# Rotary steps of q and k moved ahead of their squares, and convolution taps alternated in a transformer block

## The chip, the cores and the metric

The kernel runs on one core of one Trainium2 chip. The metric is the device time of one execution in microseconds (us); for the kernel before it is the median of three runs. The engines are TensorE (PE in the profile; PEld is its weight load), VectorE (DVE), ScalarE (ACT), GpSimd (POOL) and SyncE (SP), which here issues the transfers of weights.

## The reference

One block of a hybrid network on a sequence of 256 rows of 2048 elements, in fp32: a modulation vector from `c`, a first feed-forward network (hidden width 5632), a mixer, and a second feed-forward network, each behind a normalisation and with a gated residual. The change lies in the mixer, cut here to what matters:

```python
proj = h @ w_in                        # 256 x 5120: q, k, v, conv_a, conv_g
q = apply_rope(rms_norm(q, q_norm), cos, sin)     # 8 heads x 2 maps x 64
k = apply_rope(rms_norm(k, k_norm), cos, sin)
attn = diff_attention(q, k, v, lam)    # softmax of map 0 minus lam * softmax of map 1
u = conv_a * sigmoid(conv_g)           # 256 x 1024
u = causal_depthwise_conv(u, conv_w, conv_b)      # 31 taps for each channel
u = silu(layer_norm(u))
out = concat(attn, u) @ w_out
```

## The kernel before

**Tiles of weights.** Each product with a weight matrix is made from tiles of 512 rows by 512 columns, laid out as 128 partitions x 2048. SP loads such a tile as `raw`; `w_tile` splits it in two halves of 128x1024. Of each half ACT casts a high part `whi` (L299), and DVE takes the rest, `wlo` = `raw` - `whi` (L301). PE then makes three matmuls of 128x512 for each quarter of the tile and each half `t` of the 256 rows: `whi` with the activation's high part (L323), `wlo` with that part (L327), and `whi` with the activation's low part (L328). A tile is thus 4 x 2 x 3 = 24 matmuls. `raw`, `whi` and `wlo` have four buffers each.

**The mixer.** The projection by `w_in` goes through ten chunks of 512 columns, `ci` = 0 to 9: four of the convolution, then q0, k0, q1, k1 (each half of the heads' maps) and v0, v1. A chunk is four tiles, `pc` = 0 to 3, summed into two accumulators in PSUM, one for each `t`. What follows a finished chunk is issued by `finish_mix` behind the first tile of the next one.

- For a q or k chunk that is `qk_chunk`. For each `t`, ACT makes eight squares with row sums of 128x64 from the accumulator (L908), `rstd_of` turns the sums into `rs` (DVE scales them, L147; POOL raises them to a power, L148). DVE makes the rotary step: a product with the cosines (L913), two half products with the sines (L918), and their sum (L920). For k, ACT then scales the eight heads by `rs` (L923); for q, `rs` goes into the softmax later. One tile of weights later PE transposes the result (L895), and ACT copies it out (L898 for q, L900 and L901 for k). The scores of attention (PE L946 and L949, in `attn_probs`) need the copies of k.
- For a convolution chunk, `conv_chunk` makes `u` for two tiles of 128 channels, and one tile of weights later its inner function `rest` transposes and copies it and puts the taps into the queue `bg`. A **plain tap** is one DVE instruction that multiplies and adds for one tile of channels (L838); the tap with delay 0 is made on ACT and starts the sum (L836). A **wide tap** serves four channel tiles at once: four products on ACT (L846) and one addition of 128 x 4 x up to 256 on DVE (L848). There are eight channel tiles in two blocks of four, and in each block 8 of the 31 taps are wide (`WIDE`).

**What sets the order.** `fill(n)` takes work from `bg` up to `n` units: `TAPS[ci]` units behind every tile of chunk `ci`, where a plain tap is 1 and a wide tap 3. `after_tiles(1, f)` runs `f` one tile of weights later. A scheduler then orders the instructions of each engine from these, by the order in which they are written and by what they depend on; inside `tc.high_priority(offset=SOONER)`, with `SOONER` = 150, instructions count as written that much earlier. At run time each engine goes through its own list in that fixed order, and an instruction that waits holds up all those behind it on its engine.

Of the kernel before, what the change touches and what calls it, by code (L numbers as in the profile page):

```python
# [20 lines left out]
AF = mybir.ActivationFunctionType  # L21
# [3 lines left out]
P = 128  # L25
D = 2048
S = 256
NT = 2
# [5 lines left out]
DH = 64  # L34
CK = 31
# [3 lines left out]
SOONER = 150  # L39
# [9 lines left out]
DUE = ((8, 4), (16, 6), (22, 8), (57, 16), (108, 24), (151, 32))  # L49


TAPS = (6, 5, 6, 6, 6, 6, 8, 6, 6, 6)
TAPS_OUT = 12
WIDE = tuple(range(CK - 9, CK - 1))
RMS_EPS = 1e-6
LN_EPS = 1e-5
LAM_INIT = 0.8 - 0.6 * float(np.exp(-0.3 * 0))
# [20 lines left out]
def block_kernel(ctx: ExitStack, tc: tile.TileContext, x_in, pos_in, w_ada, small, w_gu1, w_dn1,  # L78
                 w_in, w_out, w_gu2, w_dn2, out):
    nc = tc.nc  # L80
# [57 lines left out]
    for i in range(4):  # L138
        pc = acc_tile()
        for j in range(4):  # L140
            k = 4 * i + j
# [3 lines left out]
    def rstd_of(ss, n, count, eps):  # L145

        nc.vector.tensor_scalar(out=ss, in0=ss, scalar1=1.0 / count, scalar2=eps, op0=ALU.mult, op1=ALU.add)  # L147
        nc.gpsimd.tensor_tensor(out=ss, in0=ss, in1=half[:, :n], op=ALU.pow)  # L148


    bg = deque()

    def fill(n):
        while n > 0 and bg:
            units, fn = bg.popleft()
            fn()
            n -= units
# [7 lines left out]
    def after_tiles(n, fn):  # L165
        later.append([n, fn])
# [660 lines left out]
    def conv_tap(cc, i, j):  # L827
        ct = 2 * cc + i
        y = ytile[ct // 4][:, ct % 4, :]
        p0 = _COLS["convw"][0] + ct * CK + j  # L830
        w = cst[:, p0:p0 + 1]
        d = CK - 1 - j
        u = uT[cc][:, i, :S - d]
        if d == 0:
            b0 = _COLS["convb"][0] + ct
            nc.scalar.activation(out=y, in_=u, func=AF.Identity, scale=w, bias=cst[:, b0:b0 + 1])  # L836
        else:
            nc.vector.scalar_tensor_tensor(out=y[:, d:], in0=u, scalar=w, in1=y[:, d:], op0=ALU.mult, op1=ALU.add)  # L838

    def conv_wide(b, j):  # L840

        d = CK - 1 - j
        pr = blk([P, 4, S])
        for i in range(4):
            p0 = _COLS["convw"][0] + (4 * b + i) * CK + j
            nc.scalar.activation(out=pr[:, i, d:], in_=uT[2 * b + i // 2][:, i % 2, :S - d], func=AF.Identity,  # L846
                                 scale=cst[:, p0:p0 + 1])
        nc.vector.tensor_add(out=ytile[b][:, :, d:], in0=pr[:, :, d:], in1=ytile[b][:, :, d:])  # L848

    def conv_chunk(cc, accs):  # L850
        us = []
        for t in range(NT):
            sg = tmp([P, 256])
            nc.scalar.activation(out=sg, in_=accs[t][:, 256:], func=AF.Sigmoid)
            u = tmp([P, 256])
            nc.vector.tensor_mul(out=u, in0=accs[t][:, :256], in1=sg)
            us.append(u)

        def rest():
            tp = tp_tile((P, 2, S))  # L860
            for t in range(NT):
                for i in range(2):
                    nc.tensor.transpose(tp[:, i, t * P:(t + 1) * P], us[t][:, i * P:(i + 1) * P], ident)
            uT[cc] = blk([P, 2, S])
            nc.scalar.copy(out=uT[cc], in_=tp)
            if cc % 2:
                for i in range(2):
                    bg.append((0, lambda i=i: conv_tap(cc, i, CK - 1)))
                for j in WIDE:
                    bg.append((3, lambda j=j: conv_wide(cc // 2, j)))  # L870
            for j in reversed(range(CK)):
                for i in range(2):
                    if j not in WIDE and not (cc % 2 and j == CK - 1):
                        bg.append((1, lambda i=i, j=j: conv_tap(cc, i, j)))

        after_tiles(1, rest)

    qT, kz, vv, rq_of = {}, {}, {}, {}

    def qk_chunk(name, g, accs):  # L880
        gc, gs = gcs["qn" if name == "q" else "kn"]
        if name == "q":
            dst = blk([P, 4, S])
            qT[g] = dst
        else:
            dst = [blk([P, 4, S]) for _ in range(2)]
            nc.gpsimd.memset(dst[0][DH:, :, :], 0.0)
            nc.gpsimd.memset(dst[1][:DH, :, :], 0.0)
            kz[g] = dst

        def transposed(t, A):
            tp = tp_tile((P, 4, P))
            Af = A.rearrange("p h d -> p (h d)")
            for i in range(4):
                nc.tensor.transpose(tp[:, i, :], Af[:, i * P:(i + 1) * P], ident)  # L895
            ts = slice(t * P, (t + 1) * P)
            if name == "q":
                nc.scalar.copy(out=dst[:, :, ts], in_=tp)  # L898
            else:
                nc.scalar.copy(out=dst[0][:DH, :, ts], in_=tp[:DH])  # L900
                nc.scalar.copy(out=dst[1][DH:, :, ts], in_=tp[DH:])  # L901

        for t in range(NT):
            a3 = accs[t].rearrange("p (h d) -> p h d", d=DH)
            sq = tmp([P, 8, DH])
            rs = sm([P, 8], "rs8")
            for i in range(8):
                nc.scalar.activation(out=sq[:, i, :], in_=a3[:, i, :], func=AF.Square, accum_out=rs[:, i:i + 1])  # L908
            rstd_of(rs, 8, DH, RMS_EPS)
            if name == "q":  # L910
                rq_of[g, t] = rs
            A = tmp([P, 8, DH])
            nc.vector.tensor_mul(out=A, in0=a3, in1=gc[:, t, :].unsqueeze(1).to_broadcast([P, 8, DH]))  # L913
            B = tmp([P, 8, DH])
            for h2 in range(2):
                o = slice(32 * h2, 32 * h2 + 32)
                r = slice(32 - 32 * h2, 64 - 32 * h2)
                nc.vector.tensor_mul(out=B[:, :, o], in0=a3[:, :, r],  # L918
                                     in1=gs[:, t, o].unsqueeze(1).to_broadcast([P, 8, 32]))
            nc.vector.tensor_add(out=A, in0=A, in1=B)  # L920
            if name == "k":
                for i in range(8):
                    nc.scalar.activation(out=A[:, i, :], in_=A[:, i, :], func=AF.Identity, scale=rs[:, i:i + 1])  # L923
            after_tiles(1, lambda t=t, A=A: transposed(t, A))
# [185 lines left out]
    for ci in range(10):  # L1110
        p0 = 1 if ci < HOLD else 0
        accs = first[ci][2] if ci < HOLD else [acc_tile() for _ in range(NT)]
        for pc in range(p0, 4):
            if ci == 0 and pc < 3:
                for t in range(NT):
                    st.piece(pc + 1, t)
            w = w_tile(w_in[ci, pc], ci == 0 and pc <= PRE)
            if ci == 1 or ci == 0 and pc > 1:
                ada_share(1.0, 104)
            mm_tile(accs, w, act, 4 * pc, pc == 0, pc == 3)  # L1120
            if pc == p0:
                while pend:
                    finish_mix(*pend.pop(0))
            if pc == 3 and ci < 4:
                conv_chunk(ci, accs)
            fill(TAPS[ci])
            for _ in range(UNITS):
                if probs:
                    attn_probs(*probs.popleft())
                if avq:  # L1130
                    attn_av(*avq.popleft())
        if ci >= 4:
            pend.append((ci, accs))
# [20 lines left out]
    accs = {}  # L1154
# [115 lines left out]
```

## Time and profile before

| what | value |
|---|---|
| runs | 1847.14, 1847.22, 1847.72 us; median 1847.22 |
| the profiled execution | 1849.98 us, its span 1848.2 us, mean granted clock 0.998 |
| PE busy | 1822.8 us, 99% of the span |
| DVE, ACT, POOL busy | 1438.5, 934.0, 30.2 us |

Times in the trace are counted in us from the start of the span. The stretch from 780 to 1160 us holds most of the mixer; q0 is handed to DVE and ACT at 875 us, k0 at 902 us. In a line of the timeline the columns are start, time from start to end, engine, line, operation, output <- inputs, shape, how many follow each other (x4), and in brackets the idle time ahead of it and who ended that. Instructions of an engine overlap at their ends: the time from one start to the next is shorter than the time of one.

### The profile page before, as it was taken

Reading aid. Unit: us, or ns where it says so; the run is one execution under the profiler, and the core shown is the slowest. Engines: PE = TensorE matmul, PEld = TensorE weight load, DVE = VectorE, ACT = ScalarE, POOL = GpSimd, SP = SyncE. Lnnn points to the kernel's source line nnn. Section 1 sums busy time; section 2 is a strip of 40 time slices with the busy share of each in tenths; the row PEclk is TensorE's granted clock in tenths of the full one; section 3 lists DMA queues with packets and bytes.
Section 4 is the critical chain, followed back from the end, with each engine's and each line's share of the span. In section 5 each row is a group of like instructions: output and inputs, shape, how many; then the busy total and the mean of one; then the engine's idle time right before and its main releaser. Section 6 shows DMA issues by size and latency. Waiting matters only on the chain.

```text
span 1848.2 us, 21920 instructions
## 1 busy us (share of the span) xinstructions
PE 1822.8 (99%) x8247; PEld 1502.6 (81%) x8247; DVE 1438.5 (78%) x1880; ACT 934.0 (51%) x1439; POOL 30.2 (2%) x29
## 2 busy tenths in 40 slices
PE   7999999999999999999999999999999999999999
PEld 5788888888888887788788888888888888888887
DVE  7889869998898777898998768878877765544443
ACT  7554344444444434567798655664444444433332
POOL 0000000000000000000111000000000000000000
PEclk9999999999999999999999999999999999999999
DMA  9988978889899898775444457888777755555552
GB/s 377 349 308 301 348 263 319 328 317 333 321 340 362 339 356 330 273 254 179 163 156 160 167 220 297 334 335 315 279 278 277 275 189 196 182 210 211 199 211 80
DMA packets 72729, 495.91 MB, mean 268 GB/s; under 512 B 8192, under 2 KB 8624, under 8 KB 15152
## 3 DMA queue, kind: packets, MB, share of 16 engines
q1 hardware_dynamic: 72624, 494.53, 72.2%
q8 instruction: 64, 1.05, 0.2%
q14 instruction: 41, 0.34, 0.1%
HBM read 492.37 MB, written 2.12 MB: 268 GB/s over the span
## 4 chain that ended last, share of the span: by engine, by line
PE 89%; DVE 5%; ACT 2%; DMA 1%; issue 1%; POOL 0%; SPq 0%; POOLq 0%; DVEq 0%; ACTq 0%
PE acc L327 29%; PE acc L328 29%; PE acc L323 29%; DVE wlo L301 2%; DVE blk L838 1%; PE tp L658 1%; DMA blk<-in_w_gu_dram 1%; ACT whi L299 1%; PE acc L946 1%; ACT blk L846 1%; PE tp L388 0%; DVE raw L187 0%; DMA raw<-in_w_dn_dram 0%; DMA blk<-in_w_ada_dram 0%; ACT tmp L923 0%
## 5 line engine op out<-in xcount | busy, mean ns | idle before, releaser
L299 ACT CAST whi<-raw 128x1024 fp32r<-128x1024 f32 (+1 forms) x605 | 626.8, 1046 | 711.8 <-PE acc L328 563.1
L301 DVE TENSOR_TENSOR wlo<-raw,whi 128x1024 fp32r<-128x1024 f32 (+1 forms) x605 | 724.7, 1212 | 304.4 <-ACT whi L299 303.4
L327 PE MATMUL acc<-wlo,blk 128*128 128x512 f32 x2437 | 951.8, 391 | 6.3 <-DVE wlo L301 6.2
L323 PE MATMUL acc<-whi,blk 128*128 128x512 f32 x2440 | 951.8, 393 | 1.5 <-ACT blk L397 1.3
L328 PE MATMUL acc<-whi,blk 128*128 128x512 f32 x2437 | 950.8, 390 | 0.1
L327 PEld LDWEIGHTS acc<-wlo,blk 128*128 128x128 f32 x2437 | 458.3, 188 | 103.8 <-DVE wlo L301 10.4
L323 PEld LDWEIGHTS acc<-whi,blk 128*128 128x128 f32 x2440 | 458.7, 188 | 96.0 <-ACT blk L397 1.7
L328 PEld LDWEIGHTS acc<-whi,blk 128*128 128x128 f32 x2437 | 457.8, 188 | 96.3 <-DVE blk L399 0.7
L187 DVE CUSTOM_DVE_ANT_0 raw<-raw,c_bc 128x2048 f32<-128x2048 f32 x142 | 324.3, 2286 | 15.7 <-DMA raw<-in_w_ada_dram 15.4
L486 ACT COPY blk<-acc 128x512 f32<-128x512 f32 x72 | 41.8, 588 | 61.2 <-PE acc L328 58.6
L838 DVE SCALAR_TENSOR_TENSOR blk<-blk,cst,blk 128x245 f32<-128x245 f32 (+21 forms) x176 | 70.6, 460 | 0.6 <-ACT blk L836 0.5
L650 DVE TENSOR_TENSOR blk<-acc,blk 128x512 f32<-128x512 f32 x88 | 56.7, 683 | 0.0
L323 PE MATMUL acc<-blk,blk 128*128 128x512 f32 x120 | 47.5, 398 | 1.8 <-ACT blk L315 1.8
L327 PE MATMUL acc<-blk,blk 128*128 128x512 f32 x116 | 45.3, 391 | 0.2 <-DVE blk L301 0.2
L328 PE MATMUL acc<-blk,blk 128*128 128x512 f32 x116 | 45.2, 391 | 0.0
L301 DVE TENSOR_TENSOR blk<-raw,blk 128x1024 fp32r<-128x1024 f32 x28 | 33.7, 1220 | 2.4 <-ACT blk L299 2.4
L651 ACT ACTIVATE blk<-blk 128x256 f32<-128x256 f32 x88 | 32.5, 411 | 2.9 <-DVE blk L650 2.9
L652 DVE TENSOR_TENSOR blk<-blk 128x256 f32<-128x256 f32 x88 | 33.4, 418 | 0.0
L299 ACT CAST blk<-raw 128x1024 fp32r<-128x1024 f32 x28 | 28.8, 1048 | 8.4 <-DMA raw<-in_w_dn_dram 7.1
L345 DVE TENSOR_TENSOR blk<-tp,blk 128x512 fp32r<-128x512 f32 x44 | 29.9, 684 | 0.3 <-ACT blk L344 0.3
L446 ACT ACTIVATE tmp<-tp,ada,scales 128x128 f32<-128x128 f32 x36 | 14.7, 456 | 28.0 <-DVE scales L229 15.6
L323 PEld LDWEIGHTS acc<-blk,blk 128*128 128x128 f32 x120 | 22.8, 190 | 6.6 <-ACT blk L315 2.2
(162 smaller groups left out, 739.8 us busy)
## 6 DMA issues: line engine op xcount, KB each, us to landing
raw<-in_w_gu_dram SPq DMA_DIRECT2D x161, 1024.0 KB, 5.4
raw<-in_w_ada_dram SPq DMA_DIRECT2D x142, 1024.0 KB, 6.5
raw<-in_w_dn_dram SPq DMA_DIRECT2D x88, 1024.0 KB, 4.9
raw<-in_w_in_dram SPq DMA_DIRECT2D x40, 1024.0 KB, 4.8
raw<-in_w_out_dram SPq DMA_DIRECT2D x16, 1024.0 KB, 4.8
raw<-in_w_gu_dram SPq DMA_DIRECT2D x8, 768.0 KB, 5.8
blk<-in_w_gu_dram SPq DMA_DIRECT2D x10, 512.0 KB, 13.5
blk<-gate_line SPq DMA_DIRECT2D x6, 512.0 KB, 5.5
```

The source lines that it names most:

```text
L187: nc.vector.tensor_tensor_reduce(out=raw, in0=raw, in1=c_bc, scale=1.0, scalar=0.0, op0=ALU.mult, op1=ALU.add, accum_out=ada_cols[g][:, j ...
L299: nc.scalar.copy(out=hi[:, :m, :], in_=rw)
L301: nc.vector.tensor_sub(out=lo[:, :m, :], in0=rw, in1=hi[:, :m, :].bitcast(F32))
L323: nc.tensor.matmul(acc, ah, wh, start=start, stop=False)
L327: nc.tensor.matmul(acc, ah, wl, start=False, stop=False)
L328: return nc.tensor.matmul(acc, al, wh, start=False, stop=stop)
L345: nc.vector.tensor_sub(out=lo, in0=tp, in1=hi.bitcast(F32))
L486: last_part[0] = nc.scalar.copy(out=parts[c][:, t, :], in_=accs[t])
L650: nc.vector.tensor_add(out=p[:, t, :], in0=accs[t], in1=p[:, t, :])
L651: nc.scalar.activation(out=p[:, t, :256], in_=p[:, t, :256], func=AF.Silu)
L652: nc.vector.tensor_mul(out=p[:, t, 256:], in0=p[:, t, :256], in1=p[:, t, 256:])
L838: nc.vector.scalar_tensor_tensor(out=y[:, d:], in0=u, scalar=w, in1=y[:, d:], op0=ALU.mult, op1=ALU.add)
```

## The change

Three things are edited.

1. **Rotary first.** The rotary step becomes a function `rotated`, called ahead of the squares for each `t` and inside `high_priority(offset=SOONER)`.
2. **Taps.** In the first block of four channel tiles 12 taps are wide, in the second 8 as before. The taps of a chunk are queued in one list by delay: behind plain taps number 2, 5, 8, ... stands one wide tap (in the chunks that complete a block), and it counts 2.6 units. The taps with delay 0 no longer have a place of their own at the front; they come first in that list.
3. **Units.** `TAPS` holds two numbers for each chunk: units behind its first tile, and behind each other tile.

```diff
-TAPS = (6, 5, 6, 6, 6, 6, 8, 6, 6, 6)
+TAPS = ((6, 6), (5, 5), (6, 6), (6, 7), (7, 7), (2, 7), (2, 7), (2, 7), (2, 7), (4, 7))
-WIDE = tuple(range(CK - 9, CK - 1))
+WIDE = (tuple(range(CK - 13, CK - 1)), tuple(range(CK - 9, CK - 1)))
...
-            if cc % 2:
-                for i in range(2):
-                    bg.append((0, lambda i=i: conv_tap(cc, i, CK - 1)))
-                for j in WIDE:
-                    bg.append((3, lambda j=j: conv_wide(cc // 2, j)))
-            for j in reversed(range(CK)):
-                for i in range(2):
-                    if j not in WIDE and not (cc % 2 and j == CK - 1):
-                        bg.append((1, lambda i=i, j=j: conv_tap(cc, i, j)))
+            wide = WIDE[cc // 2]
+            plain = [(i, j) for j in reversed(range(CK)) for i in range(2) if j not in wide]
+            for n, (i, j) in enumerate(plain):
+                bg.append((1, lambda i=i, j=j: conv_tap(cc, i, j)))
+                if cc % 2 and n % 3 == 1 and n // 3 < len(wide):
+                    bg.append((2.6, lambda j=wide[n // 3]: conv_wide(cc // 2, j)))
...
         for t in range(NT):
             a3 = accs[t].rearrange("p (h d) -> p h d", d=DH)
+            with tc.high_priority(offset=SOONER):
+                A = rotated(t, a3)
             sq = tmp([P, 8, DH])
             rs = sm([P, 8], "rs8")
             for i in range(8):
                 nc.scalar.activation(out=sq[:, i, :], in_=a3[:, i, :], func=AF.Square, accum_out=rs[:, i:i + 1])
             rstd_of(rs, 8, DH, RMS_EPS)
             if name == "q":
                 rq_of[g, t] = rs
-            A = tmp([P, 8, DH])
...
-            if name == "k":
+            else:
                 for i in range(8):
                     nc.scalar.activation(out=A[:, i, :], in_=A[:, i, :], func=AF.Identity, scale=rs[:, i:i + 1])
             after_tiles(1, lambda t=t, A=A: transposed(t, A))
...
-            fill(TAPS[ci])
+            fill(TAPS[ci][pc > p0])
```

In the changed kernel the lines below the edits stand elsewhere: the cast is L300, `wlo` L302, the matmuls L324, L328, L329, the plain tap L839, the wide tap's products L847 and its sum L849, the transposes L893, the rotary step L903, L908, L910, the squares L920, `rstd_of` L148 and L149, the scaling of k L926, the copies L898 and L899.

**DVE behind q0.** In the kernel before, the two parts of the tile that PE works on while q0 is worked on, `wlo_6892` and `wlo_6896`, stand just ahead of these rows, with the first `rs` (L147) between; `wlo_6969` at their end is the first part of the tile behind it:

```order
L913 TENSOR_TENSOR tmp_6935<-acc_6705,gc_qn 128x512
L918 TENSOR_TENSOR tmp_6937<-acc_6705,gs_qn 128x8x32 x2
L838 SCALAR_TENSOR_TENSOR blk_5906<-blk_6417,cst,blk_5906 128x241
L920 TENSOR_TENSOR tmp_6935<-tmp_6935,tmp_6937 128x512
L147 TENSOR_SCALAR rs_1261_6942<-rs_1261_6942 128x8
L913 TENSOR_TENSOR tmp_6953<-acc_6706,gc_qn 128x512
L918 TENSOR_TENSOR tmp_6955<-acc_6706,gs_qn 128x8x32 x2
L838 SCALAR_TENSOR_TENSOR blk_5906<-blk_6417,cst,blk_5906 128x241
L920 TENSOR_TENSOR tmp_6953<-tmp_6953,tmp_6955 128x512
L838 SCALAR_TENSOR_TENSOR blk_5906<-blk_6417,cst,blk_5906 128x240 x2
L838 SCALAR_TENSOR_TENSOR blk_5906<-blk_6417,cst,blk_5906 128x239 x2
L301 TENSOR_TENSOR wlo_6969<-raw_6965,whi_6967 128x1024
```

In the changed kernel `wlo_6920` and `wlo_6924` are the two parts of the tile that PE works on while q0 is worked on:

```order
L302 TENSOR_TENSOR wlo_6920<-raw_6916,whi_6918 128x1024
L849 TENSOR_TENSOR blk_5906<-blk_6899,blk_5906 128x4x253
L903 TENSOR_TENSOR tmp_6951<-acc_6715,gc_qn 128x512
L908 TENSOR_TENSOR tmp_6953<-acc_6715,gs_qn 128x8x32 x2
L839 SCALAR_TENSOR_TENSOR blk_5906<-blk_6417,cst,blk_5906 128x230
L910 TENSOR_TENSOR tmp_6951<-tmp_6951,tmp_6953 128x512
L903 TENSOR_TENSOR tmp_6969<-acc_6716,gc_qn 128x512
L908 TENSOR_TENSOR tmp_6971<-acc_6716,gs_qn 128x8x32 x2
L839 SCALAR_TENSOR_TENSOR blk_5906<-blk_6417,cst,blk_5906 128x229
L910 TENSOR_TENSOR tmp_6969<-tmp_6969,tmp_6971 128x512
L839 SCALAR_TENSOR_TENSOR blk_5906<-blk_6417,cst,blk_5906 128x229
L302 TENSOR_TENSOR wlo_6924<-raw_6916,whi_6922 128x1024
```

Before, both parts of the tile stood ahead of the rotary step; now the second part stands behind all of it and three plain taps, and `rs` behind that.

**ACT behind k0**, from the squares of the first `t` to the first copy of k, before:

```order
L908 ACTIVATE tmp_7137,rs_1291_7138<-acc_6886 128x64 x8
L299 CAST whi_7206<-raw_7200 128x1024
L908 ACTIVATE tmp_7163,rs_1295_7164<-acc_6887 128x64 x8
L299 CAST whi_7306<-raw_7304 128x1024
L923 ACTIVATE tmp_7149<-tmp_7149,rs_1291_7138 128x64 x8
L299 CAST whi_7310<-raw_7304 128x1024
L923 ACTIVATE tmp_7175<-tmp_7175,rs_1295_7164 128x64 x8
L299 CAST whi_7410<-raw_7408 128x1024
L299 CAST whi_7414<-raw_7408 128x1024
L900 COPY blk_7133<-tp_7234 64x4x128
```

And now; the `acc` of a square is the accumulator that DVE's rotary step reads too, and in the changed program the squares wait for DVE's L908 of the same `t`:

```order
L920 ACTIVATE tmp_7174,rs_1297_7175<-acc_6914 128x64 x8
L300 CAST whi_7330<-raw_7328 128x1024
L926 ACTIVATE tmp_7168<-tmp_7168,rs_1297_7175 128x64 x8
L920 ACTIVATE tmp_7200,rs_1301_7201<-acc_6915 128x64 x8
L300 CAST whi_7334<-raw_7328 128x1024
L926 ACTIVATE tmp_7194<-tmp_7194,rs_1301_7201 128x64 x8
L300 CAST whi_7433<-raw_7431 128x1024
L300 CAST whi_7437<-raw_7431 128x1024
L898 COPY blk_7164<-tp_7259 64x4x128
```

The squares of the second `t` now stand behind the scaling of the first. On DVE, behind k0, the order is now:

```order
L302 TENSOR_TENSOR wlo_7138<-raw_7130,whi_7136 128x1024
L903 TENSOR_TENSOR tmp_7168<-acc_6914,gc_kn 128x512
L908 TENSOR_TENSOR tmp_7170<-acc_6914,gs_kn 128x8x32 x2
L839 SCALAR_TENSOR_TENSOR blk_5907<-blk_6554,cst,blk_5907 128x241
L910 TENSOR_TENSOR tmp_7168<-tmp_7168,tmp_7170 128x512
L903 TENSOR_TENSOR tmp_7194<-acc_6915,gc_kn 128x512
L908 TENSOR_TENSOR tmp_7196<-acc_6915,gs_kn 128x8x32 x2
L148 TENSOR_SCALAR rs_1297_7175<-rs_1297_7175 128x8
L839 SCALAR_TENSOR_TENSOR blk_5907<-blk_6554,cst,blk_5907 128x240
L910 TENSOR_TENSOR tmp_7194<-tmp_7194,tmp_7196 128x512
```

Before, L147 of each `t` stood ahead of that `t`'s rotary step; now the first one stands behind the products of both. At k1, PE makes two of the first `t`'s four transposes right behind the first two matmuls of the second tile (`wlo_7854`); before, all eight stood behind that tile:

```order
L324 MATMUL acc_7751<-whi_7852,blk_5956 128x512
L324 MATMUL acc_7752<-whi_7852,blk_5956 128x512
L893 MATMUL tp_7884<-cst,tmp_7791 128x128 x2
L328 MATMUL acc_7751<-wlo_7854,blk_5956 128x512
L329 MATMUL acc_7751<-whi_7852,blk_5957 128x512
```

So these two now stand 22 matmuls earlier than the rest.

More of the change, by code (lines that the diff above doesn't have):

```diff
@@ L901, in transposed, with rotated @@
                 nc.scalar.copy(out=dst[1][DH:, :, ts], in_=tp[DH:])
[L903 to L911, printed above, removed]
+        def rotated(t, a3):
             A = tmp([P, 8, DH])
@@ L920, in qk_chunk @@
             nc.vector.tensor_add(out=A, in0=A, in1=B)
-            if name == "k":
+            return A
+        for t in range(NT):
+            a3 = accs[t].rearrange("p (h d) -> p h d", d=DH)
+            with tc.high_priority(offset=SOONER):
+                A = rotated(t, a3)
+            sq = tmp([P, 8, DH])
+            rs = sm([P, 8], "rs8")
+            for i in range(8):
+                nc.scalar.activation(out=sq[:, i, :], in_=a3[:, i, :], func=AF.Square, accum_out=rs[:, i:i + 1])
+            rstd_of(rs, 8, DH, RMS_EPS)
+            if name == "q":
+                rq_of[g, t] = rs
+            else:
                 for i in range(8):
```

## Prediction

> **What bounds the kernel now.** The page comes first: how busy each engine is. Then the windows of the mixer, where the whole change lies; then the waits of PE in them.
>
> ```profile
> span 1848.2 us, 21920 instructions
> PE 1822.8 (99%) x8247; PEld 1502.6 (81%) x8247; DVE 1438.5 (78%) x1880; ACT 934.0 (51%) x1439; POOL 30.2 (2%) x29
> ```
>
> PE is busy for 99% of the span, and no matmul is added or taken away. So the change can win only what PE now loses, or make it lose more. The second row says the same of the mixer: over 780 to 1160 us, in slices of 10 us, the sum is
>
> ```profile
> sum 380.00, PE 375.65 PEld 310.35 DVE 325.86 ACT 260.90 POOL 26.78; mean PE 9.89 PEld 8.17 DVE 8.58 ACT 6.87 POOL 0.70
> ```
>
> PE is without work for 380 - 375.65 = 4.35 us there. The slices around q0 show where (columns: window, length, busy time of PE, PEld, DVE, ACT, POOL, granted clock, DMA share, GB/s):
>
> ```profile
> 860.00:870.00 10.00, 10.00 (x45) 8.26 (x44) 7.84 (x8) 9.83 (x21) 0.00 (x0) 1.00 0.33 120
> 870.00:880.00 10.00, 9.96 (x44) 7.95 (x43) 10.00 (x22) 6.92 (x36) 1.77 (x2) 1.00 0.45 147
> 880.00:890.00 10.00, 8.19 (x34) 6.47 (x33) 10.00 (x19) 5.50 (x9) 3.42 (x3) 0.83 0.45 167
> ```
>
> At 880 to 890 us PE loses 1.81 us, has 34 matmuls where a full slice has 45, and its granted clock is 0.83; DVE is full. PE's waits in 780 to 1160 us (total, times, longest):
>
> ```profile
> PE acc L327 <- DVE wlo L301: 2.0, 2, 1.8
> PE tp L388 <- DVE tmp L380: 0.9, 2, 0.6
> PE acc L985 <- ACT blk L929: 0.7, 1, 0.7
> PE acc L323 <- ACT blk L1078: 0.3, 1, 0.3
> PE acc L946 <- ACT blk L900: 0.3, 1, 0.3
> ```
>
> Those that the change can touch are the first, 2.0 us, of which 1.8 behind q0, and the last, 0.3 us at the scores behind k1; the timeline adds about 0.3 us at the scores behind k0 (below). Together 2.6 us. The others belong to norms and to attention's end, whose instructions stay.
>
> Next, DVE and PE behind q0 (timeline):
>
> ```profile
> 875.05 2.36 DVE L301 TENSOR_TENSOR wlo<-raw,whi 128x1024 fp32r<-128x1024 f32 x2
> 877.32 0.17 DVE L147 TENSOR_SCALAR rs<-rs 128x8 f32<-128x8 f32 x1
> 877.39 0.69 DVE L913 TENSOR_TENSOR tmp<-acc,gc_qn 128x512 f32<-128x512 f32 x1
> 877.99 0.75 DVE L918 TENSOR_TENSOR tmp<-acc,gs_qn 128x256 f32<-128x256 f32 x2
> 878.65 0.47 DVE L838 SCALAR_TENSOR_TENSOR blk<-blk,cst,blk 128x241 f32<-128x241 f32 x1
> 879.03 0.69 DVE L920 TENSOR_TENSOR tmp<-tmp,tmp 128x512 f32<-128x512 f32 x1
> 879.63 0.17 DVE L147 TENSOR_SCALAR rs<-rs 128x8 f32<-128x8 f32 x1
> ...
> 883.47 2.36 DVE L301 TENSOR_TENSOR wlo<-raw,whi 128x1024 fp32r<-128x1024 f32 x2
> ```
>
> ```profile
> 875.67 0.61 PE L323 MATMUL acc<-whi,blk 128*128 128x512 f32 x2
> ...
> 879.63 0.39 PE L327 MATMUL acc<-wlo,blk 128*128 128x512 f32 x1
> 879.86 0.39 PE L328 MATMUL acc<-whi,blk 128*128 128x512 f32 x1
> ...
> 881.90 1.03 PE L895 MATMUL tp<-cst,tmp 128*128 128x128 f32 x8
> 884.75 0.50 PE L327 MATMUL acc<-wlo,blk 128*128 128x512 f32 x1 [1.81 <-DVE wlo L301]
> ...
> 885.90 0.63 PE L323 MATMUL acc<-whi,blk 128*128 128x512 f32 x1
> 886.33 0.63 PE L327 MATMUL acc<-wlo,blk 128*128 128x512 f32 x1
> ```
>
> From start to start, DVE takes 1.13 us for a `wlo` (2.27 for two), 0.60 for L913 and for L920, 0.66 for the two L918, 0.38 for a tap. PE takes 0.23 us for a matmul, so 5.44 for a tile of 24. DVE reached the next tile's first `wlo` at 883.47 only, behind the rotary step and six taps; PE had nothing else. Behind that wait the spacing is 0.43 us (885.90 to 886.33), about seven matmuls long: 7 x 0.2 = 1.4 us more. So q0 costs about 1.8 + 1.4 us today.
>
> **The change part by part.**
>
> *Taps.* Four more wide taps in the first block take away 16 plain ones: DVE saves 16 x 0.38 = 6.1 us and pays four sums, ACT pays 16 products:
>
> ```profile
> 860.52 6.48 ACT L846 ACTIVATE blk<-blk,cst 128x252 f32<-128x252 f32 x16
> 862.25 1.21 DVE L848 TENSOR_TENSOR blk<-blk,blk 128x1008 f32<-128x1008 f32 x1 [0.85 <-ACT blk L846]
> ```
>
> The sums are 4 x 1.2 = 4.8 us of DVE, the products 6.5 us of ACT. Neither lies on the path: in the slice of these very rows ACT is busy 9.83 of 10 us with sixteen products in one piece, and PE still 10.00. What covers them is tiles that are cast ahead; alternating with plain taps, the products now come four at a time. I cost them at nothing, between -0.2 us (the small wait of the second `wlo`) and +1.5 us, one group of four products (6.48 / 4 = 1.6 us) ahead of a cast that PE needs.
>
> *Rotary first, q0.* Let R be the time at which the accumulators are ready (875.19, where ACT began its squares) and E the start of the next tile on PE, 875.67. By the order now, DVE makes `wlo` for the tile's first half, a wide sum, the whole rotary step with three taps, and only then `wlo` for its second half. From the first product that is 2 x (0.60 + 0.66 + 0.38 + 0.60) + 0.38 + 1.13 = 6.0 us. PE can do 12 matmuls, two more with `whi`, and eight transposes meanwhile: 14 x 0.23 + 0.87 = 4.04 us from E (the transposes' 0.87 from their 1.03 us less the overlap). The first product starts at R at the earliest, 0.48 us before E, which makes the wait 6.0 - 0.48 - 4.04 = 1.5 us; if the first `wlo` and the wide sum run past E by 0.9 us, it is 2.9. I take a start at E + 0.3, and so 2.3 us in place of 1.8. The wait moves from the next tile into this one; it does not go.
>
> *Rotary first, k0.* Here before's rows are
>
> ```profile
> 901.90 0.22 ACT L908 ACTIVATE tmp<-acc 128x64 f32<-128x64 f32 x1 [0.98 <-PE acc L328]
> ...
> 903.49 1.10 ACT L299 CAST whi<-raw 128x1024 fp32r<-128x1024 f32 x1
> ...
> 906.96 2.11 ACT L923 ACTIVATE tmp<-tmp,rs 128x64 f32<-128x64 f32 x8
> 908.88 1.12 ACT L299 CAST whi<-raw 128x1024 fp32r<-128x1024 f32 x1
> 910.37 2.03 ACT L923 ACTIVATE tmp<-tmp,rs 128x64 f32<-128x64 f32 x8 [0.37 <-DVE tmp L920]
> 912.30 2.21 ACT L299 CAST whi<-raw 128x1024 fp32r<-128x1024 f32 x2
> 914.42 0.57 ACT L900 COPY blk<-tp 64x512 f32<-64x512 f32 x1
> ```
>
> ```profile
> 904.00 1.64 POOL L148 TENSOR_TENSOR rs<-rs,half 128x8 f32<-128x8 f32 x1 [20.46 <-DVE rs L147]
> ```
>
> ```profile
> 913.27 1.03 PE L895 MATMUL tp<-cst,tmp 128*128 128x128 f32 x8
> ...
> 914.60 0.40 PE L328 MATMUL acc<-whi,blk 128*128 128x512 f32 x1
> 915.14 0.46 PE L946 MATMUL acc<-blk,blk 128*128 128x128 f32 x2
> ```
>
> Eight squares take 1.6 us (901.90 to 903.49), eight scalings 1.9, a cast 0.95; from L147 over POOL to ACT it is about 2.0 us. PE was just not held by the transposes, and by 0.3 us at the scores (914.60 to 915.14, less one matmul). Now, with DVE starting at 901.9: the products of the first `t` end at 903.2, its squares at 904.9, but its `rs` stands behind the second `t`'s products: 901.9 + 2 x (0.60 + 0.66) + 0.38 + 0.60 = 905.4. POOL answers at 907.4; the scaling takes until 909.4. Only then come the squares of the second `t`, until 910.95; `rs` and POOL until 913.0; its scaling until 915.0. PE wants the second four transposes at 913.27 + 0.43 = 913.7 and waits 1.3 us. The copies of k come behind two casts: 915.0 + 1.9, and the first is there at 917.5. PE, 0.45 us of transposes and four matmuls after 915.1, wants it at 916.4: 1.1 us. Sum 2.4 in place of 0.3. Less if ACT's list has slack that the rows don't show: 0 at the least; more by 0.9 if DVE starts late, as at q0.
>
> *q1* now makes both parts of the tile first: 0.1 in place of 0.2. *k1*: two transposes are wanted two matmuls into the second tile, 5.44 + 0.45 after its start and so 6.4 us after R. The first scaling ends, as at k0, 909.4 - 901.9 = 7.5 us after R: 1.1 us. The other six stand 22 matmuls later (5.0 us), about when the second scaling ends; the first pair's delay helps them. 1.1 to 2.3 us; I take 1.7 in place of 0.3.
>
> *Sum.* 2.3 + 2.4 + 0.1 + 1.7 = 6.5 us against 2.6: +3.9. One slowed stretch of 1.4 us stays, as today. The profiled execution's 1849.98 us would become 1853.9; it was 2.8 above the median, so from the median 1847.2 + 3.9 = 1851.1.
>
> **Where a rule would say otherwise.** The slice at 880 us shows 0.83 of the clock behind a wait of only 1.81 us. The Trainium skill, "TensorE: Matmul & The Clock Gate", section "HAM oscillation — how this bites in real kernels", has "no PE-idle gaps >~3.4µs" as the rule for keeping the clock. By that rule no wait named here would cost any clock; the row at 880 us is against it.
>
> **The rivals.**
> - *The clock holds.* Each wait costs its own length, since none of those at k is over 1.4 us and the one at q0 may fall otherwise. Then 1.4 us goes: 1849.7. For it: the many shorter waits at clock 1.00; against it: q0's wait gets longer, and 1.81 us was enough.
> - *The clock falls more often.* Behind k0, two waits of 1.3 and 1.1 us lie within 4 us, and behind k1 as well: one or two more stretches, 1852.5 or 1853.9. For it: the row at 880 us. Against it: no such fall in before at the scores of k0 and k1, where the waits were 0.3.
> - *Not slower: the scaling of k is in time.* The price of k rests on when the second scaling ends against 913.7. If it ends 1.3 us earlier, because DVE gives `rs` ahead of the second products or ACT overlaps its small instructions better, k0 and k1 stay at 0.3 each, and the sum is 2.3 + 0.3 + 0.1 + 0.3 = 3.0: 1847.6. If q0's wait is then the 1.5 us of its lower end and takes no clock along, it is 1847.6 - 0.8 - 1.4 = 1845.4. For it: before, DVE was idle 1.65 us for the first `rs` of k0; now it starts that much earlier:
>
> ```profile
> 903.68 0.17 DVE L147 TENSOR_SCALAR rs<-rs 128x8 f32<-128x8 f32 x1 [1.65 <-ACT tmp L908]
> ```
>
>   Against it: the order, in which the squares of the second `t` stand behind the scaling of the first.
> - *Wide taps crowd the casts.* 1.5 us at one or two places in the third and fourth chunks: 1852.6 to 1854.1. Against it: the slice at 860 us.
>
> **How the numbers follow.** 0.2% is 3.7 us, about what a measurement of this kernel can tell from no change: below 1843.5 is faster, above 1850.9 slower. The forecast, 1851.1, has 0.40, and lies so near the bound that half of it is slower. The clock holds 0.14 (same), falls more often 0.18 (slower), the scaling of k in time 0.22 (0.14 same; 0.08 for a gain beyond 1843.5, if q0's wait goes as well and other waits with it), crowding 0.06 (slower). That is faster 0.08, same 0.20 + 0.14 + 0.14 = 0.48, slower 0.20 + 0.18 + 0.06 = 0.44. The range goes from 1845.4, the lower end of the k rival, to 1854.5, two more slow stretches with 0.6 us more at q0.
>
> **What would show it.** Right: PE waits inside the first tile behind q0, at L328 for the second `wlo` (L302), of about 2.3 us; at the transposes L893 behind k0, for ACT's L926, about 1.3; at the scores L949, for L898, about 1.1; at k1's first two transposes over 1. Wrong: no wait at L893; DVE's `rs` (L148) of k0 less than 3 us after the first product; or PE waiting for casts (L300) among the convolution's chunks. A gain of over 3.7 us would mean that PE lost more in the mixer than the waits above show.

## The result, and where the time went

The changed kernel takes 1861.72 us (median of six runs, 1858.56 to 1864.99) beside 1847.47 of the kernel before: the ratio estimated from the runs is 1.007, 95% interval 1.0059 to 1.0082. It is slower, the direction of the forecast, but by 14 us and not by 4, and above the range, which ended at 1854.5. The six runs form two groups, 1858.56 to 1859.23 and 1864.21 to 1864.99; the profile is of a run of the second.

The page after, its first two rows:

```profile
span 1862.9 us, 21928 instructions
PE 1828.1 (98%) x8247; PEld 1504.7 (81%) x8247; DVE 1435.6 (77%) x1868; ACT 941.0 (51%) x1455; POOL 36.7 (2%) x29
```

DVE's work fell and ACT's rose by a few us, as the taps say. The odd one is POOL: 36.7 us in place of 30.2, with the same 29 instructions. PE has more to wait for. Its waits from 860 to 1000 us, q0 to k1 (total, times, longest):

```profile
PE tp L893 <- ACT tmp L926: 7.8, 2, 4.9
PE tp L893 <- DVE tmp L910: 1.6, 1, 1.6
PE acc L328 <- DVE wlo L302: 0.8, 1, 0.8
PE acc L949 <- ACT blk L898: 0.3, 1, 0.3
```

That is 10.5 us in place of 2.3 in the same stretch of before. 1.6 and 0.8 are q0. The 7.8 are the transposes of k0 (2.9) and k1 (4.9), for ACT's scaling, and 0.3 the scores behind k0. The windows show what else that cost (window, length, busy time of PE, PEld, DVE, ACT, POOL, granted clock, DMA share, GB/s):

```profile
880.00:890.00 10.00, 7.61 (x30) 5.85 (x29) 10.00 (x17) 8.60 (x33) 5.28 (x3) 0.83 0.42 135
...
910.00:920.00 10.00, 7.13 (x31) 5.14 (x30) 5.94 (x14) 7.11 (x34) 3.48 (x2) 0.88 0.30 105
920.00:930.00 10.00, 9.73 (x45) 7.82 (x44) 7.13 (x23) 8.24 (x22) 0.00 (x0) 0.77 0.36 116
...
970.00:980.00 10.00, 4.97 (x16) 3.52 (x15) 5.62 (x9) 3.83 (x18) 6.69 (x2) 0.83 0.31 105
```

At 970 to 980 us PE made 16 matmuls where a full slice has 45. From 973.4 to 974.9 us DVE, ACT and PE all stand idle, and only POOL works, which is busy for 6.69 us of the slice. Between 860 and 1000 us the granted clock is under 0.9 at three places (880, 910 to 930 and 970 us), before at one. The profiled runs differ by 1864.99 - 1849.98 = 15.0 us. The longer waits are 10.5 - 2.3 = 8.2 of them; and PE's busy time rose by 5.3 us (1828.1 from 1822.8) with as many instructions, which is matmuls at the lower clock and transposes that come at the pace of the scaling. The remaining 1.5 us were not followed.

So the question is what ACT waited for. ACT's scalings behind k0, and then POOL's powers (start, time, in brackets the idle time ahead and who ended it):

```profile
911.73 2.03 ACT L926 ACTIVATE tmp<-tmp,rs 128x64 f32<-128x64 f32 x8 [3.95 <-POOL rs L149]
917.46 2.02 ACT L926 ACTIVATE tmp<-tmp,rs 128x64 f32<-128x64 f32 x8 [1.17 <-POOL rs L149]
```

```profile
907.10 4.59 POOL L149 TENSOR_TENSOR rs<-rs,half 128x8 f32<-128x8 f32 x1 [15.94 <-DVE rs L148]
...
969.79 5.11 POOL L149 TENSOR_TENSOR rs<-rs,half 128x8 f32<-128x8 f32 x1 [13.82 <-DVE rs L148]
```

The same power over 128x8 that took 1.64 or 1.65 us at q0, k0, q1 and k1 of before takes 4.59 and 5.11 for the first halves of k0 and k1; the second halves take 1.78 and 1.79. What DVE did beside the one at k1:

```profile
969.48 0.17 DVE L148 TENSOR_SCALAR rs<-rs 128x8 f32<-128x8 f32 x1
969.55 0.47 DVE L839 SCALAR_TENSOR_TENSOR blk<-blk,cst,blk 128x243 f32<-128x243 f32 x1
969.94 1.22 DVE L302 TENSOR_TENSOR wlo<-raw,whi 128x1024 fp32r<-128x1024 f32 x1
971.07 1.20 DVE L849 TENSOR_TENSOR blk<-blk,blk 128x1004 f32<-128x1004 f32 x1
972.19 1.22 DVE L302 TENSOR_TENSOR wlo<-raw,whi 128x1024 fp32r<-128x1024 f32 x1
```

Three instructions with two inputs from SBUF each, one right behind the other, until about 973.3; the power ends at 974.90, 1.6 us later, which is all that it took before. Before, `rs` was followed by the products of the rotary step (L913, L918), which read PSUM. DVE at k1 of before, and the power beside it:

```profile
959.33 0.17 DVE L147 TENSOR_SCALAR rs<-rs 128x8 f32<-128x8 f32 x1
959.40 0.68 DVE L913 TENSOR_TENSOR tmp<-acc,gc_kn 128x512 f32<-128x512 f32 x1
960.00 0.75 DVE L918 TENSOR_TENSOR tmp<-acc,gs_kn 128x256 f32<-128x256 f32 x2
```

```profile
959.64 1.64 POOL L148 TENSOR_TENSOR rs<-rs,half 128x8 f32<-128x8 f32 x1 [12.93 <-DVE rs L147]
```

The reading to be tested: while DVE goes from one such instruction to the next without a gap, GpSimd does not get at its own inputs.

### The profile page after: what moved, and what is told of

The parts are those of the page before. It is cut to its first block, busy times and chain, and to the rows that moved or that the text cites. A ratio compares the mean times of both kernels' runs of the same rounds, so it can differ in the third digit from the quotient of the medians.

```text
span 1862.9 us, 21928 instructions
## 1 busy us (share of the span) xinstructions
PE 1828.1 (98%) x8247; PEld 1504.7 (81%) x8247; DVE 1435.6 (77%) x1868; ACT 941.0 (51%) x1455; POOL 36.7 (2%) x29
## 4 chain that ended last, share of the span: by engine, by line
PE 89%; DVE 5%; ACT 2%; DMA 2%; issue 1%; POOL 1%; SPq 0%; POOLq 0%; DVEq 0%; ACTq 0%
PE acc L328 29%; PE acc L329 29%; PE acc L324 29%; DVE wlo L302 1%; PE tp L659 1%; DVE blk L839 1%; DMA blk<-in_w_gu_dram 1%; PE acc L949 1%; POOL rs L149 1%; ACT whi L300 1%; PE tp L389 0%; DVE blk L849 0%; DVE raw L188 0%; DMA blk<-in_w_ada_dram 0%; DMA raw<-in_w_dn_dram 0%
## 5 line engine op out<-in xcount | busy, mean ns | idle before, releaser
L300 ACT CAST whi<-raw 128x1024 fp32r<-128x1024 f32 (+1 forms) x605 | 625.5, 1045 | 707.0 <-PE acc L329 572.4
L302 DVE TENSOR_TENSOR wlo<-raw,whi 128x1024 fp32r<-128x1024 f32 (+1 forms) x605 | 724.1, 1212 | 310.7 <-ACT whi L300 309.6
L328 PE MATMUL acc<-wlo,blk 128*128 128x512 f32 x2437 | 953.8, 391 | 5.0 <-DVE wlo L302 5.0
L324 PE MATMUL acc<-whi,blk 128*128 128x512 f32 x2440 | 953.2, 393 | 1.5 <-ACT blk L398 1.3
L329 PE MATMUL acc<-whi,blk 128*128 128x512 f32 x2437 | 952.5, 391 | 0.1
L328 PEld LDWEIGHTS acc<-wlo,blk 128*128 128x128 f32 x2437 | 459.2, 188 | 101.8 <-DVE wlo L302 8.7
L324 PEld LDWEIGHTS acc<-whi,blk 128*128 128x128 f32 x2440 | 459.6, 188 | 96.0 <-ACT blk L398 1.7
L329 PEld LDWEIGHTS acc<-whi,blk 128*128 128x128 f32 x2437 | 458.7, 188 | 96.4 <-DVE blk L400 0.7
L839 DVE SCALAR_TENSOR_TENSOR blk<-blk,cst,blk 128x241 f32<-128x241 f32 (+21 forms) x160 | 65.1, 460 | 0.8 <-ACT blk L837 0.5
L324 PE MATMUL acc<-blk,blk 128*128 128x512 f32 x120 | 47.0, 395 | 1.6 <-ACT blk L316 1.6
L328 PE MATMUL acc<-blk,blk 128*128 128x512 f32 x116 | 45.4, 391 | 0.4 <-DVE blk L302 0.4
L329 PE MATMUL acc<-blk,blk 128*128 128x512 f32 x116 | 45.3, 392 | 0.0
L302 DVE TENSOR_TENSOR blk<-raw,blk 128x1024 fp32r<-128x1024 f32 x28 | 33.7, 1220 | 2.3 <-ACT blk L300 2.3
L847 ACT ACTIVATE blk<-blk,cst 128x248 f32<-128x248 f32 (+11 forms) x80 | 33.2, 501 | 0.0
L300 ACT CAST blk<-raw 128x1024 fp32r<-128x1024 f32 x28 | 28.8, 1049 | 8.3 <-DMA raw<-in_w_dn_dram 7.2
L149 POOL TENSOR_TENSOR rs<-rs,half 128x8 f32<-128x8 f32 (+1 forms) x12 | 27.6, 2303 | 239.7 <-DVE rs L148 239.7
```

The costliest lines, as they stand in the source:

```text
L300: nc.scalar.copy(out=hi[:, :m, :], in_=rw)
L302: nc.vector.tensor_sub(out=lo[:, :m, :], in0=rw, in1=hi[:, :m, :].bitcast(F32))
L324: nc.tensor.matmul(acc, ah, wh, start=start, stop=False)
L328: nc.tensor.matmul(acc, ah, wl, start=False, stop=False)
L329: return nc.tensor.matmul(acc, al, wh, start=False, stop=stop)
```

## The experiments

**One edit at a time.** Three kernels take the change apart. The first has the rotary edit alone, in the kernel before; the second has the edits on the taps alone; the third is the changed kernel with this:

```diff
-            with tc.high_priority(offset=SOONER):
-                A = rotated(t, a3)
+            if name == "q":
+                with tc.high_priority(offset=SOONER):
+                    A = rotated(t, a3)
...
             else:
+                A = rotated(t, a3)
```

Rotary alone. 

> The kernel before with only the first edit, the rotary step ahead of the squares; taps and units as before. Theory A: behind k0 the power now runs beside one tensor_tensor of 0.6 us and then plain taps, so about 2.2 us; behind k1 beside four tensor_tensor in a row (0.6, 1.1, 1.1, 1.1 us), so about 5 us, and PE waits there for about 4 us and a slowed stretch: 1850 to 1855 us. Rival (rotary first costs by its order alone, whatever stands on DVE behind rs): both powers are long, and the time is that of the changed kernel, 1858 to 1865 us. Rival (the taps make the loss): within 2 us of before.

Measured: 1859.67 us, 1.0066 of before (1.0049 to 1.0083). The whole loss is in this edit. The powers are as expected, 2.38 us at k0 and 5.33 at k1, but the time is above the 1850 to 1855 that I gave: PE waits at k1 4.5 us, and a long slowed stretch follows it (0.67 in the slice from 970 us). The time alone would also fit the rival of the mere order; the powers do not, since that rival wanted both of them long.

```profile
902.45 2.38 POOL L148 TENSOR_TENSOR rs<-rs,half 128x8 f32<-128x8 f32 x1 [15.87 <-DVE rs L147]
...
963.28 5.33 POOL L148 TENSOR_TENSOR rs<-rs,half 128x8 f32<-128x8 f32 x1 [16.26 <-DVE rs L147]
```

Taps alone. 

> The kernel before with only the edits on taps: 12 wide taps in the first block, wide and plain alternating, the new units; squares and rotary in the order of before. Theory A: rs of k is followed by products that read PSUM, as before, so the powers take 1.6 to 1.8 us, and k costs 0.3 us each; behind q0 both parts of the tile now stand ahead of the rotary step, so the wait of 1.8 us there and its slowed stretch go or shrink: 1843.5 to 1848 us. Rival (the taps make the loss): over 1855 us.

Measured: 1849.48 us, 1.0005 (0.9996 to 1.0015). The taps cost nothing that can be measured, as forecast; but my hope for q0 fell, and the time is 1.5 us above the range that I gave. The wait is still there, in three pieces, and a slowed stretch with it (0.83 in the slice from 880 us):

```profile
PE tp L893 <- DVE tmp L918: 1.7, 1, 1.7
PE tp L893 <- DVE rs L148: 0.6, 1, 0.6
PE acc L328 <- DVE wlo L302: 0.4, 1, 0.4
```

Rotary first for q only, with the new taps. 

> The changed kernel with the rotary step first for q only; for k it stands behind squares and rs, as before. Theory A: the powers of k take 1.6 to 1.8 us and PE waits at k under 0.5 us each; behind q0 the wait of 2.4 us and one slowed stretch stay, so 1847 to 1850 us. Rival (the taps make the loss, or q does): over 1855 us.

Measured: 1849.13 us, 1.0004 (0.9994 to 1.0013); the powers of k are 1.64 us. So neither the taps nor q make the loss; it comes with the rotary step of k.

**The same order with another instruction.** In the changed kernel `wlo` and the wide sums become scalar_tensor_tensor, as the plain taps are; the order on DVE, ACT and PE is the same row for row in the stretch of q and k (the first of the two places is shown):

```diff
-            nc.vector.tensor_sub(out=lo[:, :m, :], in0=rw, in1=hi[:, :m, :].bitcast(F32))
+            nc.vector.scalar_tensor_tensor(out=lo[:, :m, :], in0=rw, scalar=1.0, in1=hi[:, :m, :].bitcast(F32),
+                                           op0=ALU.mult, op1=ALU.subtract)
...
```

> The changed kernel, with the same order on every engine, but the parts wlo (L302) and the wide sums (L849 of the changed kernel) made as scalar_tensor_tensor ((raw * 1.0) - whi, and the like) in place of tensor_tensor; the same numbers come out. In the changed kernel the GpSimd power behind k0 took 4.59 us and behind k1 5.11 (1.64 before), and ended 1.6 us after the last of a row of DVE tensor_tensor instructions with two inputs from SBUF, while plain taps, which are scalar_tensor_tensor, followed without holding it up. Theory A (DVE's tensor_tensor keeps GpSimd from its inputs): the powers take 1.6 to 2.3 us, PE's waits at the transposes of k fall from 2.9 and 4.9 us to 0 to 0.7 and about 1.5, one or two of the three slowed stretches at k go, and the time is 1850 to 1854 us. Theory B (the order alone makes k late, as the prediction walked it): the powers stay long for another reason and the time stays within 2 us of the changed kernel's 1858.6 to 1865. Theory C (scalar_tensor_tensor holds GpSimd up as well): as B. The Trainium skill, page SBUF — State Buffer, section Who interferes with whom, says that a DVE instruction with two SBUF inputs contends with a GpSimd instruction that reads SBUF; by the words of that rule it would be C.

Measured: 1859.83 us, 1.0064 (1.0043 to 1.0086): theory A in that form falls, theory C holds. The power of k1 is the same to the last digit, beside instructions of the other kind:

```profile
962.66 5.11 POOL L149 TENSOR_TENSOR rs<-rs,half 128x8 f32<-128x8 f32 x1 [13.79 <-DVE rs L148]
```

So it makes no difference which of the two instructions stands there; what they share is two inputs from SBUF. Plain taps have two such inputs too and let the power in more easily (last section), so the two inputs are not the whole story. Behind k0 the power took 1.72 us here, and I could not say from this kernel alone whether the edit did that. The unedited kernel took 1.72 there too, in an execution shown below.

**A gap for GpSimd.** Behind `rs` of k, one DVE instruction more that reads PSUM; its result isn't used. The power writes to a tile of its own here. Before, it wrote in place and took 1.64 us, so that is not what shortens it.

```diff
...
+                ms, rs = rs, sm([P, 8], "rs8")
+                nc.vector.tensor_scalar(out=ms, in0=ms, scalar1=1.0 / DH, scalar2=RMS_EPS, op0=ALU.mult, op1=ALU.add)
+                nc.gpsimd.tensor_tensor(out=rs, in0=ms, in1=half, op=ALU.pow)
+                with tc.high_priority(offset=SOONER):
+                    nc.vector.tensor_mul(out=sq, in0=a3, in1=ms.unsqueeze(2).to_broadcast([P, 8, DH]))
...
```

> The changed kernel with one DVE instruction more for each half of k: behind the scaling of the row sums (L148) and one plain tap, a product of the accumulator in PSUM with rs, 128x512, one input from SBUF; nothing uses its result. GpSimd's power writes to a tile of its own. DVE has 0.6 us more to do at four places. Theory A (DVE instructions with two SBUF inputs, one behind the other, keep GpSimd from its inputs; one with its input in PSUM lets it in): the power of the first half of k0 and of k1 takes 1.7 to 2.0 us (4.59 and 5.11 in the changed kernel), PE's wait at the transposes of k1 falls from 4.9 to about 1.5 to 2.5 us, a slowed stretch goes, and the kernel is faster than the changed one although it does more: 1851 to 1855 us. Theory B (the order alone makes k late): the powers stay long, 1859 to 1866 us.

Measured: 1854.5 us, 1.0031 (1.0019 to 1.0043). More work, and 4 to 10 us less than the changed kernel. DVE behind k1, and the power beside it:

```profile
962.90 0.16 DVE L926 TENSOR_SCALAR rs<-rs 128x8 f32<-128x8 f32 x1
962.97 0.46 DVE L839 SCALAR_TENSOR_TENSOR blk<-blk,cst,blk 128x243 f32<-128x243 f32 x1
963.35 0.68 DVE L929 TENSOR_TENSOR tmp<-acc,rs 128x512 f32<-128x512 f32 x1
963.95 1.19 DVE L849 TENSOR_TENSOR blk<-blk,blk 128x1004 f32<-128x1004 f32 x1
```

```profile
963.20 1.73 POOL L927 TENSOR_TENSOR rs<-rs,half 128x8 f32<-128x8 f32 x1 [10.65 <-DVE rs L926]
```

The power ends at 964.93, 1.58 us behind the start of L929: 1.73 us with it, 5.11 without, although the wide sum and both `wlo` still follow one another behind it. PE's longest wait at the transposes of k falls from 4.9 to 1.5 us:

```profile
PE tp L893 <- ACT tmp L931: 1.7, 2, 1.5
```

So the hold-up depends on what DVE reads beside the power. Not all of the loss goes with it: 1.0031 of before is left, with one slowed stretch at k1 (0.83 in the slice from 960 us). How much of that is the new order and how much the four added instructions, this run doesn't tell.

**Without GpSimd.** In the changed kernel, for q and k; this gives 1/x where the kernel needs 1/sqrt(x), so only its time is of use:

```diff
-            rstd_of(rs, 8, DH, RMS_EPS)
+            nc.vector.tensor_scalar(out=rs, in0=rs, scalar1=1.0 / DH, scalar2=RMS_EPS, op0=ALU.mult, op1=ALU.add)
+            nc.vector.reciprocal(out=rs, in_=rs)
```

> The changed kernel with GpSimd's power for q and k replaced by a reciprocal on DVE; what it computes is 1/x in place of 1/sqrt(x) there, so the result of attention is another, and its time is that of a chain without GpSimd. The rotary step stays first. Theory A (GpSimd, held up, makes the greater part of the loss): PE's wait at the transposes of k0 is under 0.5 us, at k1 0.5 to 1.5, at the scores of k0 0.3 to 1; 1848 to 1852 us. Theory B (the order alone): the waits fall by the 1.6 us of a power at most, to 1.3 and 3.3 us; 1854 to 1860 us.

Measured: 1849.78 us, 1.0004 (0.9995 to 1.0014), with the rotary step first for q and k. Its waits from 860 to 1000 us:

```profile
...
PE tp L893 <- ACT tmp L927: 0.5, 2, 0.4
```

q0 is the same, 1.6 and 0.8; of k, 0.5 us is left. With GpSimd out of the chain the new order costs nothing that can be measured. That takes away the power's own 1.64 us along with the hold-up, so it is not the price of the order with an undisturbed power; the run with the gap is nearer to that.

**The two groups.** The changed kernel ran twice more.

> The changed kernel once more, to see another execution in the trace: its six runs fell into two groups, 1858.6 to 1859.2 and 1864.2 to 1865.0, and the profiled one was of the second. In the run with scalar_tensor_tensor, of the first group, the power of the first half of k0 took 1.72 us, having started 0.15 us ahead of the end of a plain tap; in the changed kernel's profile it started 0.14 us ahead of the same end and took 4.59. If that race makes the two groups, an execution of about 1859 us has a power of about 1.7 us behind k0 and one slowed stretch less, and one of about 1864 us has 4.6 us again; behind k1 it is 5.1 us in both.

> The changed kernel a third time, for an execution of the other group. If it takes about 1859 us, the power of the first half of k0 should take about 1.7 us, against 4.59 in the two executions of 1864 and 1865 us, and PE's wait at the transposes of k0 fall from 2.9 to under 1 us; if about 1864 us, 4.6 again.

Measured: 1863.9 us with a power of 4.59 us at k0, and 1859.05 us with one of 1.72; 5.11 at k1 in both. The execution of 1859 us, DVE and POOL at k0:

```profile
904.66 0.16 DVE L148 TENSOR_SCALAR rs<-rs 128x8 f32<-128x8 f32 x1
904.73 0.46 DVE L839 SCALAR_TENSOR_TENSOR blk<-blk,cst,blk 128x240 f32<-128x240 f32 x1
905.11 0.69 DVE L910 TENSOR_TENSOR tmp<-tmp,tmp 128x512 f32<-128x512 f32 x1
905.72 2.35 DVE L302 TENSOR_TENSOR wlo<-raw,whi 128x1024 fp32r<-128x1024 f32 x2
```

```profile
904.97 1.72 POOL L149 TENSOR_TENSOR rs<-rs,half 128x8 f32<-128x8 f32 x1 [14.74 <-DVE rs L148]
```

And the one of 1865 us at the same place:

```profile
906.79 0.17 DVE L148 TENSOR_SCALAR rs<-rs 128x8 f32<-128x8 f32 x1
906.86 0.47 DVE L839 SCALAR_TENSOR_TENSOR blk<-blk,cst,blk 128x240 f32<-128x240 f32 x1
907.24 0.68 DVE L910 TENSOR_TENSOR tmp<-tmp,tmp 128x512 f32<-128x512 f32 x1
907.84 2.35 DVE L302 TENSOR_TENSOR wlo<-raw,whi 128x1024 fp32r<-128x1024 f32 x2
...
910.11 1.22 DVE L839 SCALAR_TENSOR_TENSOR blk<-blk,cst,blk 128x240 f32<-128x240 f32 x3
```

The power starts 0.14 us ahead of L910 in both (904.97 and 905.11; 907.10 and 907.24). In the one it gets in there and ends 1.58 us behind that point; in the other it misses, and the next chance is the plain taps at 910.11, 1.58 us ahead of its end at 911.69. In hundredths of a microsecond the trace shows no difference ahead of that point, so this looks like a race. The four traced executions with this row agree that it parts the runs into two groups, 5 us apart: 4.59 us in those of 1865 and 1864 us, 1.72 in that of 1859 us and in the run with scalar_tensor_tensor (1857.81 us). The others were not traced.

**Other units alone.** The wait behind q0 comes from DVE's queue, so I took taps away there alone, from the kernel before (`fill(TAPS[ci][pc > p0])` as in the change):

```diff
-TAPS = (6, 5, 6, 6, 6, 6, 8, 6, 6, 6)
+TAPS = ((6, 6), (5, 5), (6, 6), (6, 6), (6, 5), (0, 6), (9, 9), (6, 6), (6, 6), (6, 6))
```

> The kernel before with other units of taps alone: behind the first tile of q0 none (6 before), behind the tiles of the last convolution chunk 6, 5, 5, 5, in the tiles of k0 9 (8 before), elsewhere 6 or 5 as before. In the order, both wlo parts of the tile behind q0 then stand ahead of or between the rotary steps, and the transposes of q0 stand a tile later. If the 1.8 us of waiting behind q0 and its slowed stretch of 1.4 us come from DVE's queue of taps there, both go and nothing takes their place: 3 us under before, 1844.5 to 1846.5 us beside 1848.7. Rival: the wait moves to the next tile or to k0, within 1 us of before.

Measured: 1846.33 us beside 1848.25, 0.9989 (0.998 to 0.9998): 1.9 us faster than the kernel before, with an interval that only just leaves out 1, and 15 us under the changed one. (One of its eleven runs took 4752 us, with no counterpart in any other; the comparison leaves it out, and its cause is not known.) The 1.8 us behind q0 are gone, but not without a price: from 860 to 1000 us PE now waits once, behind q1, and the slice that had a clock of 0.83 has 1.00:

```profile
PE acc L327 <- DVE wlo L301: 1.2, 1, 1.2
```

```profile
880.00:890.00 10.00, 10.00 (x50) 8.34 (x49) 10.00 (x19) 6.60 (x10) 2.78 (x3) 1.00 0.51 196
```

The last step was to ease q1 in the same way, with (4, 6) for its chunk and (7, 7) for the last. 

> The last kernel of the units with q1 eased as well: 4 units behind the first tile of q1 and 6 behind its others, 7 in the last chunk. There PE waited 1.2 us for wlo in the run with new units, behind the rotary step of both halves and five taps; two taps fewer stand there now, so 0.4 to 0.6 us. Time 0.3 to 1 us under that run, 1845 to 1846.3 us beside 1848.3 for before. Rival: the taps moved to k1 and v make a wait of their own, no gain.

Measured: 1851.52 us, 1.0016 (1.0007 to 1.0025), slower than before. PE's wait for `wlo` behind q1 is 0.4 us now (1.1 in all, less the longer one of 0.7, which lies elsewhere), but new waits came behind the scores, the longest at the transposes of attention's end (780 to 1160 us, in part):

```profile
PE tp L1000 <- ACT tmp L995: 3.2, 1, 3.2
PE acc L327 <- DVE wlo L301: 1.1, 2, 0.7
PE acc L323 <- ACT whi L299: 0.6, 1, 0.6
```

No gain, as the rival beside it had it. The longest of the new waits is not for a tap, though: ACT's L995 waits for a power of GpSimd, beside which DVE makes two `wlo` in a row:

```profile
1000.40 2.35 DVE L301 TENSOR_TENSOR wlo<-raw,whi 128x1024 fp32r<-128x1024 f32 x2
```

```profile
1000.57 3.05 POOL L148 TENSOR_TENSOR rs<-rs,half 128x4 f32<-128x4 f32 x1 [40.48 <-DVE rs L147]
```

```profile
1003.65 1.14 ACT L995 ACTIVATE tmp<-acc,rs 128x128 f32<-128x128 f32 x4 [2.12 <-POOL rs L148]
```

The same power took 1.16 us in the kernel of the step before, where two plain taps followed `rs`. It looks like the same hold-up at a second place, 3.05 - 1.16 = 1.9 of the 3.2 us by this estimate; no run tests it there. The kernel before has it as well, 3.05 us at 999.91, but no wait of PE at L1000 is listed there.

## Why the prediction was wrong

*Taps at nothing.* Right: 1.0005 with the taps alone. The rival "wide taps crowd the casts" fell: in the changed kernel no wait of PE for a cast (L300) is listed from 780 to 1160 us.

*q0.* The total is right, 2.3 us forecast for the wait within the first tile and 1.6 + 0.8 measured, in every kernel with the rotary step first for q and the new taps. The place is right only in part: all of it was to be at L328 for the second `wlo`, where 0.8 are, and 1.6 are at the transposes, for the sum of the rotary step (L910). Nor is the rotary step its cause by itself: with it alone PE lost 1.8 us there, as before, and with the taps alone 2.7. That the sum came so close is partly luck.

*q1.* Right: no wait is listed there now.

*k0.* Right in the execution of 1859 us. PE at k0 in that execution:

```profile
912.51 0.92 PE L893 MATMUL tp<-cst,tmp 128*128 128x128 f32 x5
913.59 1.28 PE L893 MATMUL tp<-cst,tmp 128*128 128x128 f32 x3 [0.15 <-ACT tmp L926]
914.62 0.48 PE L324 MATMUL acc<-whi,blk 128*128 128x512 f32 x1
...
917.00 0.46 PE L949 MATMUL acc<-blk,blk 128*128 128x128 f32 x2 [1.20 <-ACT blk L898]
```

The eight transposes last from 912.51 to 914.62, 2.1 us in place of the 0.8 of before, since the last of them come at the pace of the scaling: 1.3 us more, 1.3 forecast, though as a wait, of which only 0.15 is listed. At the scores 1.20, 1.1 forecast. In the executions of 1864 and 1865 us the power is 2.9 us longer, and PE's wait at the transposes is 2.9 where it was 0.15.

*k1.* This is where it failed in every execution: 1.7 us forecast, 4.9 measured, and the upper bound was 2.3. The step is the one at k0 that k1 took over: "from L147 over POOL to ACT it is about 2.0 us". I took the 1.64 us of the power from rows in which DVE read PSUM right behind L147, and applied them to an order in which `rs` is followed by `wlo` and a wide sum. The order stood before me; I asked what the chain waits for on its own engines and not what runs beside it on the neighbour. The runs put 5.11 us in its place. With the gap it is 1.73, and with GpSimd out of the chain the transposes of k wait 0.5 us in all. For the execution of 1859 us this one step nearly closes the sum, by an estimate: 3.9 us forecast, 4.9 - 1.7 = 3.2 more at k1, and 1.7 more of lost clock (0.86 and 0.80 in the slices from 960 and 970 us, against 0.83 in one slice of before) make 8.8; its span is 1857.1 - 1848.2 = 8.9 us longer.

*The clock.* I kept one slowed stretch. The profiled execution of 1865 us has them at q0, at k0 and at k1, as in the rival "the clock falls more often", which had priced one or two more; "the clock holds" fell. Its reason was another, though: waits of 1.3 and 1.1 us at k0, which in the run of 1859 us left the clock at 1.00 there, where the ones that cost a stretch were of 2.9 and 4.9.

*The rivals.* "The scaling of k is in time" fell, and with it the time on the other side. The one that was needed was not among them: that the work which stands beside GpSimd changes, and not only the order of the chain. The Trainium skill has a rule for such a pair, in "SBUF — State Buffer", section "Who interferes with whom": a DVE instruction with two SBUF inputs contends with a GpSimd instruction that reads SBUF. The trace agrees, 5.11 us beside 1.64. With a power that ends 1.6 us after the last of three such instructions of 1.13 us, as the rows show it, k1 would have come out 3 x 1.13 = 3.4 us higher, at 5.1 us; that is an estimate from the rows above.

## What to carry to other kernels

A duration read from a trace holds for what ran beside it. Before an instruction is moved, look at both sides of the pair that share something: here a GpSimd step of 1.6 us became one of 5 because the DVE instructions behind its trigger changed from PSUM readers to SBUF readers. One instruction that reads PSUM brought the power back to 1.73 us; to leave the trigger of k where PSUM is read next brought the time back as well (1849.13 us). And where the engine that sets the time waits for a queue, take work out of that queue at that place rather than reorder the chain: other numbers in one table won 1.9 us here, where the three edits lost 14. Even so, the next step by the same rule lost again, at a place that the numbers were not meant to touch.

## What was not expected of the hardware

- GpSimd gets in at some joints of DVE's row and not at others. Its power ended 1.58 us behind the start of a row of plain taps in the run of 1865 us (910.11 and 911.69), whose third operand, a scalar for each partition, is read from SBUF, but not between `wlo`, wide sum and `wlo`. Why a tap leaves an opening was not tested.
- A wait and its slowed stretch are loosely tied. The same 1.6 + 0.8 us behind q0 was followed by a granted clock of 0.83 in the run of 1865 us, and in the run of 1859 us the slice has 1.00 (of the seven traced executions with these two waits, three have 0.83 and four 1.00):

```profile
880.00:890.00 10.00, 8.05 (x35) 6.24 (x36) 10.00 (x15) 8.61 (x29) 6.17 (x4) 1.00 0.52 175
```
